# Output projection of a hybrid attention layer: four of eight pairs as two couples of seven block products

## The chip, the core and the metric

One core of a Trainium2 chip runs the kernel. The metric is the time of one execution on the device, in microseconds (us). The engines work in parallel, each through its own instructions in order: PE multiplies matrices (PEld loads its stationary operand), DVE and ACT do element work, POOL does too, SP issues most of the transfers (DMAs) between the chip's memory and the on-chip buffers. An instruction waits for semaphores that others raise; while it waits, everything behind it on its engine waits as well.

## The reference

A layer of 1024 rows (positions) and width 1024. The input is normalised and modulated, goes through one input projection, then through eight heads of forgetting attention and eight of stick-breaking attention; the gated head outputs `y` (1024 x 1024) go through the output projection, are multiplied by a gate per column, added to the scaled input and normalised. The part that the change touches:

```python
y = jnp.concatenate([y_fox, y_sb], axis=-1) @ w_out[layer]
resid = DEEPNORM_ALPHA * x + gate[:, None, :] * y
x = _layer_norm(resid, ln_g[layer], ln_b[layer])
```

## The kernel before

**Pairs and stages.** The sixteen heads are eight pairs; a pair is 128 of the 1024 inner columns of `y`. All large matmuls are done three times: each float operand is split into a rounded high part and the rest (`hi`, `lo`), and a product is yh by hi, yl by hi, yh by lo, summed in PSUM. A loop over 128 attention units (8 pairs, 2 heads, 8 blocks of 128 rows) writes the code; the matmuls of later projections are put between the units as fillers (`FILL` says how many steps for each pair), and in pair 7 the first output products are (`TAIL`). The order on each engine follows the order in which the code is written, with a few edges added (`after`).

**Weights.** `gen_split_out` runs beside the fillers from pair 4 on: for 16 pieces of `w_out` (128 x 512) it loads the piece, multiplies it by the gate on POOL, makes hi and lo on POOL (`fetch_w`, L125 and following) and stores both in `wo_dr`. `load_wo` loads them back when the last input projection lets go of the `u` and `v` buffers.

**The value buffers** (tag `v`, three of 8 KB per partition) hold the values of a pair's heads; at some times one of the three has no tenant.

**The tail.** Row tiles are taken in the order 6, 7, 4, 5, 2, 3, 0, 1, each in two halves of 512 columns (the last tile in 512, 256, 256). For one half, `o_step` (L937 to L939) adds the three products of all eight pairs in one PSUM accumulator (tag `acc`, two buffers). The y rows of pairs 0 to 6 were stored in `y_dr`; `load_y` reloads a row tile into `wraw` (two buffers, shared with weight pieces) and POOL makes hi (L917) and lo (L918) in the ring of five (`RING`). Pair 7 stays on chip (`y7h`, `y7l`). `o_half` then adds the scaled input on DVE (L956; `xr`, 512 KB, has four buffers of its own, tag `k`), takes the statistics (L957), and at the row's end `ln_finish` (L192 on DVE, L194 and L195 on POOL) and two DVE passes for each half (L964, L968) finish the row, which SP stores. The last tile shares the second pass with ACT and POOL (L971, L972).

Of the kernel before, what the change touches and what calls it, by code (L numbers as in the profile page):

```python
# [13 lines left out]
P = 128  # L14
# [13 lines left out]
def tile_hybrid_layer(  # L28
# [17 lines left out]
    nc = tc.nc  # L46

# [33 lines left out]
    SPACE = 10  # L81
    BEHIND = 1

# [26 lines left out]

    y_dr = dr.tile([NPAIR, P, SEQ], F32, tag="y_dr", name="y_dr")
    wo_dr = dr.tile([2, NPAIR, P, D], F32, tag="wo_dr", name="wo_dr")
# [4 lines left out]

    def ring_w(key):
        return [sb.tile([P, 528], F32R, tag=tag, bufs=RING, name=f"{tag}_{key}") for tag in ("whi", "wlo")]
# [26 lines left out]
    def load_x(t):  # L146
        if t == 6:
            late_x.append(pt_tile("x_67", F32))
        xi = att_tile(f"x_{t}") if t < 6 else late_x[0][:, t - 6, :]
        nc.sync.dma_start(xi, x[t * P:(t + 1) * P, :])  # L150
        xt.append(xi)
# [306 lines left out]
    masks, scaled, lows, gates = [], [], [], []  # L458
# [11 lines left out]
    def att_scores(u, following):  # L470
# [30 lines left out]
        else:  # L501
# [18 lines left out]
            nc.gpsimd.tensor_tensor(be[:, :ke - 1], be[:, :ke - 1], kp[:, 1:ke], op=ALU.mult)  # L520
# [24 lines left out]
    y_last, summed = [], []  # L545
# [15 lines left out]
    def att_sum(acc, p, h, j):  # L561
# [9 lines left out]
        if p == NPAIR - 1:  # L571
            if not y_last:
                y_last.extend([big("sg", 2, "y7h", F32R), big("kl", 2, "y7l", F32R)])
            yh, yl = y_last
            nc.scalar.copy(yh[r, qs], yt[r, :])
            nc.gpsimd.tensor_tensor(yl[r, qs], yt[r, :], yh.bitcast(F32)[r, qs], op=ALU.subtract)
        else:
            nc.sync.dma_start(y_dr[p, r, qs], yt[r, :])

# [303 lines left out]
    def load_wo(pr):  # L883
        hi = big(f"u{pr}", 1, f"woh_{pr}", F32R)
        lo = big(f"v{pr}", 1, f"wol_{pr}", F32R)
        nc.sync.dma_start(hi.bitcast(F32), wo_dr[0, pr])
        nc.sync.dma_start(lo.bitcast(F32), wo_dr[1, pr])
        wo[pr] = (hi, lo)

    def gen_split_out():  # L890
        for pr in range(NPAIR):
            for h in range(2):
                s = slice(h * 512, h * 512 + 512)
                with after(*scaled[BEHIND:BEHIND + 1]):
                    hi, lo = fetch_w(f"o{pr}_{h}", w_out[pr * P:(pr + 1) * P, s], 512, gate[:, s])
                nc.sync.dma_start(wo_dr[0, pr, :, s], hi.bitcast(F32)[:, :512])
                nc.sync.dma_start(wo_dr[1, pr, :, s], lo.bitcast(F32)[:, :512])
                for _ in range(SPACE):
                    yield
# [8 lines left out]
    y_t = {}  # L908

    def load_y(t):  # L910
        ts_ = slice(t * P, (t + 1) * P)
        for p0, n in ((0, 4), (4, 3)):
            raw = raw_tile(f"yr_{t}_{p0}")[:, :n * P]
            nc.sync.dma_start(raw.rearrange("p (a q) -> p a q", q=P),
                              y_dr[p0:p0 + n, :, ts_].rearrange("a p q -> p a q"))
            hi, lo = y_t[t, p0 // 4] = ring_w(f"y_{t}_{p0}")
            nc.gpsimd.tensor_scalar(hi[:, :n * P], raw, 1.0, 1.0, op0=ALU.mult, op1=ALU.mult)  # L917
            nc.gpsimd.tensor_tensor(lo[:, :n * P], raw, hi.bitcast(F32)[:, :n * P], op=ALU.subtract)  # L918

    o_acc = {}  # L920
    OUT_ORDER = (6, 7, 4, 5, 2, 3, 0, 1)

    def groups(t):
        return ((0, 512), (512, 768), (768, 1024)) if t == OUT_ORDER[-1] else ((0, 512), (512, 1024))

    def o_step(t, h, pr):
        if pr == 0:
            o_acc[t, h] = (t_tile if h == 2 else acc_tile)(f"o_{t}_{h}")
        acc = o_acc[t, h]
        if pr == NPAIR - 1:  # L930
            yh, yl = (v[:, t * P:(t + 1) * P] for v in y_last)
        else:
            yh, yl = (v[:, pr % 4 * P:][:, :P] for v in y_t[t, pr // 4])
        hi, lo = wo[pr]
        s = slice(*groups(t)[h])
        acc = acc[:, :s.stop - s.start]
        nc.tensor.matmul(acc, yh, hi[:, s], start=(pr == 0), stop=False)  # L937
        nc.tensor.matmul(acc, yl, hi[:, s], start=False, stop=False)  # L938
        nc.tensor.matmul(acc, yh, lo[:, s], start=False, stop=(pr == NPAIR - 1))  # L939

    res = {}

    def o_half(t, h):
        ts_ = slice(t * P, (t + 1) * P)
        s = slice(*groups(t)[h])
        ng = len(groups(t))
        if h == 0:
            xr = big("k", 4, f"xr_{t}")
            nc.sync.dma_start(xr, x[ts_, :])
            res[t] = (att_tile(f"r_{t}"), xr, sb.tile([P, 3, 6], F32, tag="st", bufs=3, name=f"st_b{t}")[:, :ng, :])  # L950
        r, xr, st = res[t]
        last = t == OUT_ORDER[-1]

        acc = o_acc[t, h][:, :s.stop - s.start]
        to = acc if last else r[:, s]
        nc.vector.scalar_tensor_tensor(to, xr[:, s], ALPHA, acc, op0=ALU.mult, op1=ALU.add)  # L956
        nc.vector.bn_stats(st[:, h, :], to)  # L957
        if h == ng - 1:
            mv, rs = ln_finish(st, f"b{t}")
            cuts = [slice(*g) for g in groups(t)]  # L960
            mid = [o_acc[t, j][:, :c.stop - c.start] if last else r[:, c] for j, c in enumerate(cuts)]

            def first(j):
                nc.vector.scalar_tensor_tensor(mid[j], mid[j], mv[:, 0:1], lgb[0][:, 0, cuts[j]],  # L964
                                               op0=ALU.subtract, op1=ALU.mult)

            def second(c, m):
                nc.vector.scalar_tensor_tensor(r[:, c], m, rs[:, 0:1], lgb[0][:, 1, c], op0=ALU.mult, op1=ALU.add)  # L968

            def shared(c, m):  # L970
                nc.scalar.activation(r[:, c], m, AF.Copy, scale=rs[:, 0:1])  # L971
                nc.gpsimd.tensor_tensor(r[:, c], r[:, c], lgb[0][:, 1, c], op=ALU.add)  # L972

            if not last:
                for j in range(2):
                    first(j)
                    second(cuts[j], mid[j])
                    if t not in OUT_ORDER[:2]:
                        nc.sync.dma_start(out[ts_, cuts[j]], r[:, cuts[j]])
                if t in OUT_ORDER[:2]:  # L980
                    nc.sync.dma_start(out[ts_, :], r)
                return
            for j in (1, 0, 2):
                first(j)
            shared(cuts[1], mid[1])
            c = cuts[2]
            cut = c.stop - 96
            shared(slice(cut, c.stop), mid[2][:, cut - c.start:])
            second(cuts[0], mid[0])
            second(slice(c.start, cut), mid[2][:, :cut - c.start])  # L990
# [4 lines left out]
    def gen_out_first(t):  # L995
        for h in range(2):
            for pr in range(NPAIR - 1):
                o_step(t, h, pr)
                yield
# [200 lines left out]
```

## Time and profile before

| what | value |
|---|---|
| median of 3 runs | 680.6 us (680.34 to 680.93) |
| span of the profiled execution | 678.6 us |
| median above that span | 2.0 us |
| POOL busy, 600 to 672 us | 29.48 us |
| DVE busy, 600 to 672 us | 41.30 us |

The span is the time from the first to the last event that the profiler recorded on the core; the device time adds a little around it. Busy times are in us; in a list of groups a row gives line, engine, operation, output and inputs, shape, count, then busy time, mean in ns, and idle time ahead with what ended it. A row of the timeline gives start, duration, engine, line and operation. In the list of transfers the last number is the median time from issue to landing.

### The profile page before, as it was taken

To read this page: it belongs to the slowest core of one execution; us is meant where nothing else is said; L and a number is where in the kernel's file an instruction comes from. 1 tells how busy PE (TensorE), PEld (TensorE's weight loads), DVE (VectorE), ACT (ScalarE), POOL (GpSimd) and SP (SyncE) were. 2 spreads that over 40 slices of the span, in tenths; PEclk is the share of its full clock that TensorE was granted. 3 is DMA by queue.
4 is the path that set the end of the run, shared out by engine and by line. 5 is a ranking of instruction groups with operands and counts; after the bars stand their busy time and mean duration, and the time that the engine had idled before them with its cause. 6 is when DMAs were issued, how large, how long until landed. Compare 5 with 4: busy or idle time off the path is not lost.

```text
span 678.6 us, 11231 instructions
## 1 busy us (share of the span) xinstructions
PE 668.3 (98%) x3713; PEld 571.2 (84%) x3713; DVE 485.9 (72%) x1001; ACT 382.6 (56%) x889; POOL 405.2 (60%) x530
## 2 busy tenths in 40 slices
PE   8999999999999999999999999999999999999995
PEld 4888898888998888889988888889988888888885
DVE  6787779868677777686776675766676777775645
ACT  5576468757567667576675564655565766521000
POOL 5560279755357556556378878785785365655412
PEclk9999999999999999999999999999999999999998
DMA  9983432112101112122124555263452297153301
GB/s 326 401 312 126 139 79 75 41 28 67 29 20 56 54 42 57 40 54 56 49 93 144 151 164 174 87 201 112 127 169 59 70 350 302 59 177 107 120 32 63
DMA packets 46474, 81.55 MB, mean 120 GB/s; under 512 B 5264, under 2 KB 20176, under 8 KB 46416
## 3 DMA queue, kind: packets, MB, share of 16 engines
q1 hardware_dynamic: 44832, 76.37, 35.1%
q10 hardware_dynamic: 1584, 4.47, 2.1%
q8 instruction: 29, 0.48, 0.3%
q14 instruction: 29, 0.24, 0.1%
HBM read 60.34 MB, written 16.29 MB: 113 GB/s over the span
## 4 chain that ended last, share of the span: by engine, by line
PE 97%; DMA 1%; DVE 0%; POOL 0%; ACT 0%; issue 0%; SPq 0%; POOLq 0%
PE m L312 11%; PE m L314 10%; PE m L313 10%; PE pv L554 10%; PE T L537 9%; PE S L484 5%; PE S L483 5%; PE o L939 4%; PE o L937 4%; PE o L938 4%; PE v L370 4%; PE v L372 4%; PE v L371 4%; PE st_q L647 1%; PE st_k L647 1%; PE st_late L647 1%
## 5 line engine op out<-in xcount | busy, mean ns | idle before, releaser
L540 DVE TENSOR_TENSOR pt<-T,pt 128x512 fp32r<-128x512 f32 (+2 forms) x192 | 102.7, 553 | 43.8 <-ACT pt L539 42.2
L539 ACT CAST pt<-T 128x512 fp32r<-128x512 f32 (+2 forms) x192 | 88.9, 479 | 64.5 <-PE T L537 62.5
L312 PE MATMUL m<-uh,whi 128*128 128x512 f32 x304 | 123.3, 405 | 0.1
L314 PE MATMUL m<-uh,wlo 128*128 128x512 f32 x304 | 119.8, 394 | 0.0
L313 PE MATMUL m<-ul,whi 128*128 128x512 f32 x304 | 119.7, 394 | 0.0
L520 POOL TENSOR_TENSOR be<-be,kp 128x127 f32<-128x127 f32 (+3 forms) x64 | 78.9, 1234 | 36.2 <-DVE kp L518 24.4
L554 PE MATMUL pv<-pt,v 128*128 128x512 f32 x320 | 82.8, 388 | 0.0
L514 DVE TENSOR_TENSOR_SCAN kp<-kp,floor 128x128 f32<-128x128 f32 (+3 forms) x64 | 58.6, 915 | 17.6 <-ACT kp L506 17.4
L499 POOL TENSOR_SCALAR a<-a,l 128x1024 f32<-128x1024 f32 (+3 forms) x64 | 48.4, 756 | 34.3 <-DVE l L497 26.0
L483 PE MATMUL S<-k,q 128*128 128x512 f32 (+5 forms) x192 | 68.8, 360 | 0.0
L314 PEld LDWEIGHTS m<-uh,wlo 128*128 128x128 f32 x304 | 57.1, 188 | 13.7
L496 ACT ACTIVATE a<-a,nm 128x1024 f32<-128x1024 f32 (+3 forms) x64 | 49.8, 779 | 28.6 <-DVE nm L491 28.1
L312 PEld LDWEIGHTS m<-uh,whi 128*128 128x128 f32 x304 | 57.2, 188 | 10.2 <-PE T L537 0.3
L484 PE MATMUL S<-kl,qz 128*128 128x512 f32 (+5 forms) x192 | 65.2, 341 | 0.0
L313 PEld LDWEIGHTS m<-ul,whi 128*128 128x128 f32 x304 | 57.3, 188 | 9.0
L554 PEld LDWEIGHTS pv<-pt,v 128*128 128x128 f32 x320 | 55.5, 189 | 8.9
L570 POOL TENSOR_TENSOR ty<-ty,sg 64x256 f32<-64x256 f32 x64 | 46.9, 733 | 23.4 <-issue 12.2
L491 DVE CUSTOM_DVE_ANT_0 a<-S,fb 128x1024 f32<-128x1024 f32 (+3 forms) x64 | 48.2, 753 | 16.9 <-PE S L484 12.0
L456 ACT CAST qz<-q 64x128 fp32r<-64x128 f32 x128 | 37.3, 296 | 34.2 <-PE S L484 33.0
L506 ACT ACTIVATE kp<-S 128x384 f32<-128x384 f32 (+4 forms) x96 | 44.0, 494 | 21.5 <-PE S L484 20.2
L370 PE MATMUL v<-whi_v,uh 128*128 128x256 f32 (+1 forms) x192 | 54.7, 285 | 0.0
L372 PE MATMUL v<-wlo_v,uh 128*128 128x256 f32 (+1 forms) x192 | 54.2, 282 | 0.0
(296 smaller groups left out, 1628.3 us busy)
## 6 DMA issues: line engine op xcount, KB each, us to landing
raw<-in_w_qkg_dram SPq DMA_DIRECT2D x38, 256.0 KB, 2.7
wss<-in_w_ss_dram SPq DMA_DIRECT2D x14, 512.0 KB, 8.1
x<-in_x_dram SPq DMA_DIRECT2D x8, 512.0 KB, 7.1
k<-k SPq DMA_DIRECT2D x32, 128.0 KB, 2.3
wg<-in_w_gate_dram SPq DMA_DIRECT2D x8, 512.0 KB, 4.9
raw_o<-in_w_out_dram SPq DMA_DIRECT2D x16, 256.0 KB, 3.0
fb<-f_dr ACTq DMA_DIRECT2D x8, 512.0 KB, 4.5
wo_dr<-whi_o SPq DMA_DIRECT2D x16, 256.0 KB, 2.1
```

The source lines that it names most:

```text
L312: nc.tensor.matmul(acc, hi[:, c], u_hi[kt][:, s], start=(kt == 0), stop=False)
L313: nc.tensor.matmul(acc, hi[:, c], u_lo[kt][:, s], start=False, stop=False)
L314: nc.tensor.matmul(acc, lo[:, c], u_hi[kt][:, s], start=False, stop=(kt == NB - 1))
L370: nc.tensor.matmul(acc[:, :n], u_hi[kt][:, ts_], hi[:, s], start=(kt == 0), stop=False)
L372: nc.tensor.matmul(acc[:, :n], u_hi[kt][:, ts_], lo[:, s], start=False, stop=(kt == NB - 1))
L483: nc.tensor.matmul(S[:, s, :w], qst[p][h][:, qs], kst[p][h][:, ks], start=True, stop=False)
L484: nc.tensor.matmul(S[:, s, :w], z, klo[p][:, ks], start=False, stop=True)
L520: nc.gpsimd.tensor_tensor(be[:, :ke - 1], be[:, :ke - 1], kp[:, 1:ke], op=ALU.mult)
L537: nc.tensor.transpose(tp[:, b * P:(b + 1) * P], a[:, kb * P:(kb + 1) * P], ident)
L539: nc.scalar.copy(hi[:, :n, qo:qo + P], t3)
L540: lows[:] = [nc.vector.tensor_tensor(lo[:, :n, qo:qo + P], t3, hi.bitcast(F32)[:, :n, qo:qo + P], op=ALU.subtract)]
L554: nc.tensor.matmul(acc2[:, :, q0:], vt[p][:, kb, h * P:(h + 1) * P], pt[:, :, q0:], start=(kb == 0), stop=(kb == last))
```

## The change

Pairs 0 to 3 become two couples. Within a couple, y of a pair of row tiles is a 2 x 2 block matrix A (row tile by pair), the gated weights a 2 x 2 block matrix B (pair by column half), and the 2 x 2 result is had by seven block products instead of eight, from sums and differences of blocks:

- the early products A11 B11, S2 T2, S3 T3, S1 T1, each into an accumulator of its own over both couples; ACT and DVE add them up in an SBUF tile `e_t` of each row;
- the late products P4 = A22 T4, P2 = A12 B21, P3 = S4 B22, each in one accumulator with the plain products of pairs 4 to 7 for that half (12 matmuls); the half that gets no late product is `gen_22`.

The row pairs are (6,7), (4,5), (2,3), (0,1), numbered 0 to 3. The operands (S and T blocks, hi and lo) are made by `gen_operands` in the value buffer without tenant, in the fill steps that `ROOMS` names, which are steps of pairs 2 and 3 for couple 0 and of pairs 4 and 5 for couple 1, and are stored in `wo_dr`, `ye_dr`, `yl_dr`. `gen_plain` splits the weights of pairs 4 to 7 as before (eight pieces). Each half's residual is now a load of 256 KB into `wraw`, a scaling on ACT and an add on POOL into `e_t`; the accumulator is added on DVE (`half_add`). A finished row is stored as one piece of 512 KB, and for its first half ACT and POOL make the second pass (`shared`). The y rows of pairs 4 to 6 are loaded as before, three blocks of 128 for a row tile instead of seven; rows 7, 5 and 3 at set steps, rows 6, 4, 2, 1, 0 behind all late loads.

```diff
-    SPACE = 10
+    STAY = 14
+    SPACE = 12
+    ROOMS = ((126, 226), (264, 366))
+    NC = 2
+    ROWS = ((6, 7), (4, 5), (2, 3), (0, 1))
+    EARLY = (("A11", "B11"), ("S2", "T2"), ("S3", "T3"), ("S1", "T1"))
+    LATE = {"P4": ("A22", "T4"), "P2": ("A12", "B21"), "P3": ("S4", "B22")}
...
+    def ring_set(key):
+        return sb.tile([P, 2, 528], F32R, tag="w", bufs=RING, name=f"w_{key}")
...
+    def halves(raw, n, key):
+        both = rooms[now()][:, 2:]
+        nc.scalar.copy(both[:, 0, :n], raw[:, :n])
+        with tied():
+            nc.gpsimd.tensor_tensor(both[:, 1, :n], raw[:, :n], both.bitcast(F32)[:, 0, :n], op=ALU.subtract)
+        return both.bitcast(F32)
...
+    def weight_piece(c, q):
...
+            nc.gpsimd.tensor_tensor(r4, r4, both, op=ALU.mult)
...
+        both = halves(raw, 3 * P, f"ob_{c}_{q}")
...
+        less(b11, b12, b11)
+        less(b12, b22, b12)
+        less(b22, b22, b11)
+        less(b21, b21, b22)
+        yield
+        both = halves(raw, 4 * P, f"ot_{c}_{q}")
...
+    def load_y(row):
+        n = NPAIR - 1 - 2 * NC
+        raw = raw_tile(f"yr_{row}")[:, :n * P]
...
+        hi, lo = y_row[row] = ring_w(f"y_{row}")
+        nc.gpsimd.tensor_scalar(hi[:, :n * P], raw, 1.0, 1.0, op0=ALU.mult, op1=ALU.mult)
+        nc.gpsimd.tensor_tensor(lo[:, :n * P], raw, hi.bitcast(F32)[:, :n * P], op=ALU.subtract)
...
+    def residual(t, x, h):
+        r = ROWS[t][x]
+        xr = raw_tile(f"xr_{t}_{x}_{h}")[:, :512]
+        nc.sync.dma_start(xr, x_in[r * P:(r + 1) * P, h * 512:h * 512 + 512])
+        nc.scalar.activation(xr, xr, AF.Copy, scale=ALPHA)
+        nc.gpsimd.tensor_tensor(half_of(t, x, h), half_of(t, x, h), xr, op=ALU.add)
...
+    def half_add(t, x, h, acc):
+        e = half_of(t, x, h)
+        nc.vector.tensor_tensor(e, e, acc, op=ALU.add)
+        stats(t, x, h, e)
...
+    def row_end(t, x):
+        r, row = e_t[t][x], ROWS[t][x]
+        mv, rs = ln_finish(o_st[t, x][:, :2, :], f"b{t}{x}")
+        for h in range(2):
+            c = slice(h * 512, h * 512 + 512)
+            first(r[:, c], c, mv)
+            (shared if h == 0 else second)(r, c, r[:, c], rs)
+        nc.sync.dma_start(out[row * P:(row + 1) * P, :], r)
...
+    def gen_late(t, which, x, h):
+        residual(t, x, h)
+        acc = (t_tile if which == "P2" else acc_tile)(f"o_{t}_{which}")
+        yield from block(t, 1, LATE[which], acc, ends=(True, False))
+        yield from plain(t, x, slice(h * 512, h * 512 + 512), acc, ends=(False, True))
+        half_add(t, x, h, acc)
+        if which != "P2":
+            row_end(t, x)
...
-    tail = chain([gen_out_first(6), gen_out_last(6)] + [gen_out(t) for t in OUT_ORDER[1:]])
+    tail = chain([gen_early(0), gen_early(1), gen_22(0), gen_22(1), gen_early(2), gen_early(3), gen_22(2),
+                  *(gen_late(t, "P4", 1, 0) for t in range(3)),
+                  gen_late(0, "P2", 0, 0), gen_late(1, "P2", 0, 0),
+                  gen_late(0, "P3", 0, 1), gen_late(1, "P3", 0, 1),
+                  gen_late(2, "P2", 0, 0), gen_late(2, "P3", 0, 1),
+                  gen_22(3), gen_late(3, "P4", 1, 0), gen_late(3, "P2", 0, 0), gen_end(3)])
...
+        if k == LAST + 15:
...
+            for row in (6, 4, 2, 1, 0):
+                load_y(row)
```

**What the order of the instructions says.** POOL in the middle of the tail, before (`whi_y` and `wlo_y` are the split y rows, `rs_b5` the reciprocal root of row tile 5):

```order
L570 TENSOR_TENSOR ty_7_1_0_7446<-ty_7_1_0_7446,sg_7_6538 64x256
L917 TENSOR_SCALAR whi_y_0_0_7493<-yr_0_0_7491 128x512
L576 TENSOR_TENSOR y7l_6798<-ty_7_1_0_7446,y7h_6797 64x256
L918 TENSOR_TENSOR wlo_y_0_0_7494<-yr_0_0_7491,whi_y_0_0_7493 128x512
L194 TENSOR_SCALAR rs_b5_7469<-mv_b5_7467 128x1
L195 TENSOR_TENSOR rs_b5_7469<-rs_b5_7469,mhalf_89 128x1
```

The same place after (`w_y_1` is the split y row tile 1, `xr_0_1_0` the residual of row pair 0, second row, first half; `e0_1` the sum tile of that row, `rs_b01` its reciprocal root):

```order
L1058 TENSOR_SCALAR w_y_2_7456<-yr_2_7454 128x384
L1059 TENSOR_TENSOR w_y_2_7456<-yr_2_7454,w_y_2_7456 128x384
L1058 TENSOR_SCALAR w_y_1_7461<-yr_1_7459 128x384
L1059 TENSOR_TENSOR w_y_1_7461<-yr_1_7459,w_y_1_7461 128x384
L1100 TENSOR_TENSOR e0_1_6897<-e0_1_6897,xr_0_1_0_7488 128x512
L215 TENSOR_SCALAR rs_b01_7515<-mv_b01_7513 128x1
L216 TENSOR_TENSOR rs_b01_7515<-rs_b01_7515,mhalf_89 128x1
L1100 TENSOR_TENSOR e1_1_7071<-e1_1_7071,xr_1_1_0_7524 128x512
L1120 TENSOR_TENSOR e0_1_6897<-e0_1_6897,lngb_6698 128x512
```

The adds of residuals (L1100) and the shared second pass (L1120) are new on POOL, and the first residual of the late group stands behind the split of row 1.

SP, the transfers at that place, after (`yr_` are y rows, `xr_` residuals, both in `wraw`):

```order
L1055 DMA yr_2_7454<-y_dr_91 128x3x128
L1055 DMA yr_1_7459<-y_dr_91 128x3x128
L1055 DMA yr_0_7464<-y_dr_91 128x3x128
L1098 DMA xr_0_1_0_7488<-in_x_dram 128x512
L1098 DMA xr_1_1_0_7524<-in_x_dram 128x512
L1098 DMA xr_2_1_0_7564<-in_x_dram 128x512
L1129 DMA out_0_dram<-e0_1_6897 128x1024
```

The residuals of the late group are issued behind all five y rows, in the same two buffers: xr_0_1_0 in that of yr_1, xr_1_1_0 and the next two in that of xr_0_1_0, until yr_0 is split.

DVE, after, at the end of the first late products (`o_0_P4` is an accumulator):

```order
L1109 TENSOR_TENSOR e0_1_6897<-e0_1_6897,o_0_P4_7492 128x512
L1105 BN_STATS st_b01_7238<-e0_1_6897 128x6
L213 BN_AGGR mv_b01_7513<-st_b01_7238 128x2
L1113 SCALAR_TENSOR_TENSOR e0_1_6897<-e0_1_6897,mv_b01_7513,lngb_6698 128x512 x2
L1116 SCALAR_TENSOR_TENSOR e0_1_6897<-e0_1_6897,rs_b01_7515,lngb_6698 128x512
L1109 TENSOR_TENSOR e1_1_7071<-e1_1_7071,o_1_P4_7528 128x512
```

Before, the first of these six was L956, which took the residual straight from its own buffer. Now the add that frees an accumulator stands behind the second pass of the row ahead, and it reads an `e` tile to which POOL has added the residual.

Late in the tail on POOL, after (`rs_b10` belongs to row pair 1, first row, whose sum tile is `gate`):

```order
L215 TENSOR_SCALAR rs_b10_7725<-mv_b10_7723 128x1
L1100 TENSOR_TENSOR e3_0_7346<-e3_0_7346,xr_3_0_0_7852 128x512
L216 TENSOR_TENSOR rs_b10_7725<-rs_b10_7725,mhalf_89 128x1
L1120 TENSOR_TENSOR gate_88<-gate_88,lngb_6698 128x512
```

A residual of the last row pair stands between the two operations of a root that an earlier row waits for.

More of the change, by code (lines that the diff above doesn't have):

```diff
@@ L578, in att_sum @@
             nc.sync.dma_start(y_dr[p, r, qs], yt[r, :])
+            stored.add((p, h, j))
     def chain(gens):
@@ new lines, in tied, with less, now @@
+    def tied():
+        return after(*(scaled[BEHIND:BEHIND + 1] or prods))
+    def halves(raw, n, key):
[4 more added lines that the diff above has]
+        return both.bitcast(F32)
+    def less(to, a, b, op=ALU.subtract):
+        nc.vector.tensor_tensor(to, a, b, op=op)
+    rooms, handed = {}, [0]
+    def now():
+        return [i for i, (a, b) in enumerate(ROOMS) if a <= done[0] < b][0]
@@ L941, in tile_hybrid_layer @@
[L941 to L990, printed above, removed]
-            nc.scalar.dma_start(out[ts_, cuts[0]], r[:, cuts[0]])
-            rest = slice(cuts[1].start, c.stop)
-            nc.sync.dma_start(out[ts_, rest], r[:, rest])
```

318 lines of the change are left out of this document (242 added, 76 removed).

## Prediction

> **What bounds the kernel now.** The page comes first, for the busy shares and the chain; then the busy time by stage, to see whether the chain's answer holds in each stage; then the waits of PE.
>
> ```profile
> span 678.6 us, 11231 instructions
> PE 668.3 (98%) x3713; PEld 571.2 (84%) x3713; DVE 485.9 (72%) x1001; ACT 382.6 (56%) x889; POOL 405.2 (60%) x530
> PE 97%; DMA 1%; DVE 0%; POOL 0%; ACT 0%; issue 0%; SPq 0%; POOLq 0%
> ...
> 219.00:311.00 92.00, 92.00 (x478) 77.40 (x477) 70.97 (x109) 62.57 (x144) 56.92 (x80) 1.00 0.20 50
> 349.00:440.00 91.00, 91.00 (x466) 76.40 (x465) 61.49 (x154) 52.02 (x121) 73.32 (x82) 1.00 0.44 134
> 600.00:672.00 72.00, 71.46 (x336) 58.72 (x334) 41.30 (x73) 4.13 (x13) 29.48 (x37) 1.00 0.27 95
> ...
> PE sc_all L179 <- POOL ident masks.py:199: 1.5, 1, 1.5
> PE xT_early L256 <- ACT x L222: 0.9, 1, 0.9
> PE st_q L647 <- ACT uh L270: 0.4, 1, 0.4
> ```
>
> PE makes 97% of the chain. In the stage rows (window, length, then busy us of PE, PEld, DVE, ACT, POOL, then clock) it is busy all the time, in the attention stages as in the output projection; in the last window the missing half microsecond is only the time after the last matmul. Its list of waits is three entries long, all in the start. So a matmul that goes is worth its whole time, and any new wait of PE costs its whole length: nothing is slack.
>
> **What the products save.** Before, the projection has 360 matmuls of 512 columns and 48 of 256; after, 342 and 36 (a couple takes 7 block products of 3 matmuls for a pair of row tiles where two pairs took 8). So 18 of 512 and 12 of 256 go.
>
> ```profile
> 619.25 0.39 PE L937 MATMUL o<-woh,whi_y 128*128 128x512 f32 x1
> 619.48 0.40 PE L938 MATMUL o<-woh,wlo_y 128*128 128x512 f32 x1
> 619.72 0.40 PE L939 MATMUL o<-wol,whi_y 128*128 128x512 f32 x1
> ...
> 620.65 0.39 PE L937 MATMUL o<-woh,whi_y 128*128 128x512 f32 x1
> ...
> 670.35 0.28 PE L938 MATMUL o<-woh,wlo_y 128*128 128x256 f32 x1
> ...
> 671.18 0.28 PE L939 MATMUL o<-wol,y7h 128*128 128x256 f32 x1
> ```
>
> A matmul's duration (0.39) overlaps the next one; the price is from start to start: 1.40 over the six steps from 619.25 to 620.65, 0.233 each, and 0.83 over the seven from 670.35 to 671.18, 0.1186 each for 256 columns. 18 x 0.233 + 12 x 0.1186 = 4.19 + 1.42 = **5.6 us saved**. The last matmul starts at 671.18 and the span ends at 678.6; that ending of 7.4 us has the same operations in both kernels, so it is carried over.
>
> **First stall: the residual halves share a two-buffer pool with the y rows.** The tail's n-th matmul stands after the change where the n-th stood before, so the times above are also those that the new one would have if it waited for nothing. The third product of the late group (o_2_P4) would start at 620.65. It needs the accumulator of o_0_P4, which DVE frees with the add into e0_1; that add follows POOL's add of the residual xr_0_1_0; its transfer follows, in its buffer, yr_1, which POOL frees with its two operations on w_y_1; and these write the ring set that held row 5, last read by the ninth plain matmul of o_1_P4. That one stands at 619.72 and ends at 620.11. So the chain starts half a microsecond before PE needs its end.
>
> ```profile
> 611.36 0.39 PE L939 MATMUL o<-wol,whi_y 128*128 128x512 f32 x1
> ...
> 611.84 0.51 POOL L917 TENSOR_SCALAR whi_y<-yr 128x384 fp32r<-128x384 f32 x1 [2.49 <-PE o L939]
> 612.44 1.01 POOL L918 TENSOR_TENSOR wlo_y<-yr,whi_y 128x384 fp32r<-128x384 f32 x1
> ...
> raw<-in_w_qkg_dram SPq DMA_DIRECT2D x38, 256.0 KB, 2.7
> xr<-in_x_dram SPq DMA_DIRECT2D x8, 512.0 KB, 3.5
> out_dram<-r SPq DMA_DIRECT2D x11, 256.0 KB, 2.0
> ...
> L633 ACT CAST hw<-raws 128x512 fp32r<-128x512 f32 x5 | 3.1, 623 | 3.3 <-DMA raws<-in_w_qkg_dram 3.3
> L125 POOL TENSOR_TENSOR raw_o<-raw_o,gate 128x512 f32<-128x512 f32 x16 | 20.7, 1294 | 6.6 <-DMA raw_o<-in_w_out_dram 6.6
> L956 DVE SCALAR_TENSOR_TENSOR r<-xr,o 128x512 f32<-128x512 f32 x14 | 9.5, 686 | 19.2 <-PE o L939 18.6 <-POOL whi_y L917 0.5
> ```
>
> The same release exists before: matmul at 611.36, end 611.75, POOL's copy at 611.84, so 0.09 us for the hop, 0.51 and 1.01 for the two operations with 0.09 between. Then the transfer, 256 KB: 2.7 us to landing for the like load of weights (between 2.0, that of an output store, and 3.5, the 512 KB load); ACT's scaling 0.62; POOL's add 1.29; DVE's add 0.69; three hops of 0.09. Sum: 0.09 + 0.51 + 0.09 + 1.01 + 2.7 + 0.62 + 1.29 + 0.69 + 0.27 = 7.3, from 620.11 to 627.4, and the signal to PE makes it 627.5. Against 620.65 that is **6.9 us of idle PE** (6.2 to 7.7 with the two other transfers). Behind POOL's wait for w_y_1 stand all later POOL operations of the tail, so nothing of this can be overtaken.
>
> The Trainium skill, "DMA: Bandwidth & Descriptors" (Anatomy of one DMA), says that a transfer has about 2 us of fixed cost, mostly the receipt of its last byte. The rows agree, with 2.0 us for 256 KB as the shortest; by 2 us alone the stall would be 6.2.
>
> **Second stall: one turn of a buffer is longer than a product.** A product of 18 matmuls takes 18 x 0.233 = 4.2 us. Thirteen halves still need their residual then, one for each product of the late group; a turn of its buffer is 2.7 + 0.62 + 1.29 and hops, 4.8 us. Until POOL has split w_y_0, the other buffer is taken by yr_0, so four residuals go through a single buffer, one every 4.8 us. POOL also carries, per row, two operations on the reciprocal root and one shared add, and runs them in order.
>
> ```profile
> L964 DVE SCALAR_TENSOR_TENSOR r<-r,mv_b,lngb 128x512 f32<-128x512 f32 x14 | 10.9, 818 | 0.2
> L968 DVE SCALAR_TENSOR_TENSOR r<-r,rs_b,lngb 128x512 f32<-128x512 f32 x14 | 10.1, 748 | 3.2 <-POOL rs_b L195 3.2
> L194 POOL TENSOR_SCALAR rs_b<-mv_b 128x1 f32<-128x1 f32 x8 | 4.9, 607 | 22.7 <-DVE mv_b L192 21.6 <-DVE l L497 0.8
> L195 POOL TENSOR_TENSOR rs_b<-rs_b,mhalf 128x1 f32<-128x1 f32 x8 | 6.7, 831 | 0.6
> ```
>
> I followed the engines' orders by these durations from POOL's first residual add, done at 626.7: the adds for rows' halves end at 631.5, 636.2, 641.7, 644.6, 647.2, 649.4, 652.0, 654.2, 656.7, 659.3, 661.4. The last of these (e3_0) stands ahead of the power operation for row 10's root; DVE's second pass over `gate` waits for that (662.2 to 662.95), and the add that frees o_2_P3's accumulator stands behind it on DVE: done 663.7. o_3_P4 takes that accumulator. After the first stall PE would reach it 140 instructions after 627.5, at 660.1. The working gives 3.6 us; with 0.1 us for each of the some eight hops that I left out, 4.5. I take **4.4 us**. The bounds are 2 (transfers of 2.2 us) and 6 (of 3.0): some eight transfers follow one another, and each adds its difference.
>
> **Smaller terms.** All have a gain excluded, since PE has no idle time that they could take away, so they start at nothing. (a) o22_3 waits for the add of o_1_P3: 0.25. (b) The last early product of each row pair is read by two DVE adds of 0.69, the next but one product may start only behind them, and one product of 6 matmuls is 1.4 long: 0 to 0.5, taken 0.3. (c) T4's second weight block is loaded where the last score product's k buffer was (its matmuls end at 606.0) and is read at 612.86.
>
> ```profile
> 605.76 0.27 PE L484 MATMUL S<-kl,qz 128*128 128x128 f32 x1
> woh<-wo_dr SPq DMA_DIRECT2D x8, 512.0 KB, 8.1
> ```
>
> Alone such a 512 KB load takes 3.5 us, in a queue of them 8.1, so 0 to 1.3; taken 0.3. (d) The operand pieces in pairs 2 and 3 add to POOL, for the eight pieces of a couple, 4 x 1.29 + 8 x 1.02 + 8 x 1.30 = 23.7 us, to DVE 32 operations, to ACT 16 casts.
>
> ```profile
> L918 POOL TENSOR_TENSOR wlo_y<-yr,whi_y 128x384 fp32r<-128x384 f32 x6 | 6.1, 1020 | 0.4
> L379 DVE TENSOR_TENSOR v<-v,v 128x128 fp32r<-128x128 f32 x60 | 17.0, 285 | 8.8 <-ACT v L378 8.0
> ```
>
> By the window 219 to 311, POOL goes from 56.9 to 80.6 of 92 us and DVE (32 x 0.285 = 9.1) from 71.0 to 80.1: it fits, but a unit whose weights pass through POOL's in-order queue may come up to 1.3 us late. 0 to 3, taken 0.45, as most pieces are tied behind the unit's own operation. In pairs 4 and 5, POOL loses eight of the sixteen split pieces and gains the same 23.7: nothing. Together (a) to (d): **1.3 us**.
>
> **The clock.** An idle PE has a price of its own. In the tail the granted clock falls soon after the last matmul, and the first matmuls of the program, of one form, are slower than the later ones:
>
> ```profile
> 670.00:675.00 5.00, 1.46 (x13) 1.25 (x11) 3.40 (x8) 0.82 (x2) 1.58 (x4) 0.85 0.00 0
> 675.00:679.00 4.00, 0.00 (x0) 0.00 (x0) 0.18 (x1) 0.00 (x0) 0.26 (x1) 0.50 0.35 133
> L179 PE MATMUL sc_all<-ident 128*128 128x512 f32 x8 | 5.1, 802 | 1.5 <-POOL ident masks.py:199 1.5
> L179 PE MATMUL sc_all<-ident x8: 592/648/1222, 1.5 to 6.1; 128*128 128x512 f32 x8
> ```
>
> 0.85 over five microseconds is 1.5 us at half clock, so it fell about 2 us after PE stopped. The eight first matmuls are busy for 5.1 us, against 8 x 0.592 = 4.7 if all were as fast as the fastest (0.4 more), and by their mean they are 8 x (0.802 - 0.592) = 1.7 longer; so a restart costs 0.4 to 1.7 us. After the first stall that loss is made up, because the residual chain runs on and PE waits for it at o_3_P4 anyway; after the second it is not: 0 to 1.7, **0.8 taken**.
>
> The Trainium skill, "TensorE: Matmul & The Clock Gate" (The HAM clock gate), speaks against every gap: PE falls to half clock after an idle window of about 3.4 us and needs about 3.4 us of work to come back. The rows of the end agree on the fall, to 0.50. By that rule both stalls would be followed by half speed, the sum that the third rival below takes.
>
> **Sum.** 678.6 - 5.6 + 6.9 + 4.4 + 1.3 + 0.8 = 686.4 us of span; the median of the runs shown, 680.6, lies 2.0 above the profiled span, so **688.4 us**, slower by 1.1%.
>
> **Rivals.**
> - *Only the first stall is seen.* If transfers land in 2.2 us and the hops are short, the residuals catch up with PE: 680.6 - 5.6 + 6.4 + 1.1 = 682.5. For it: out stores of the same size land in 2.0. Against: every load row is at 2.7 or more, and POOL's own sequence is nearly as long as PE's.
> - *The block products come through.* One mechanism: the ring set of row 5 is free before o_1_P4 reads it, so w_y_1 is split some 7 us earlier. Then stall one is gone and the residual chain is 7 us ahead, which covers stall two: 680.6 - 5.6 + 1.3 = 676.3. It decides whether POOL's copy into w_y_1 starts before or after 620. Against: row 5's set has its second reader in that product, and the order has nothing between.
> - *The clock halves after both stalls*, and the second restart follows a longer gap: 1.7 for each in place of 0.8 gives 688.4 + 2.6 = 691.0. For it the fall at the end; against it, that the first loss hides in the second wait.
> - *The attention stage becomes bound by POOL* in pairs 2 and 3 (88% busy): term (d) at 3 in place of 0.45: 691.0. Against: 11 us are left.
>
> **How the numbers follow.** Forecast 0.55 (685 to 690.5 by its bounds), first rival 0.2, second 0.06, third 0.12, fourth 0.07. The range leaves out the second rival, the low part of the first and the high part of the last two: 682.0 to 692.0. A measurement of this kernel can tell about 0.2% (1.4 us) from no change. Faster by more: 0.06. Within: 0.05, the low end of the first rival, where saving and stall cancel. Slower: 0.89.
>
> **What would show it.** Right: the list of PE's waits gets an entry of 6 to 7 us on the first matmul of o_2_P4, released by DVE's add into e0_1, and one of 2 to 6 us on o_3_P4; POOL's copy for w_y_1 starts just after the ninth plain matmul of o_1_P4; the granted clock dips near 625. Wrong: those matmuls start without a wait; the residual transfers land in far less than 2.7 us; or PE waits between 219 and 440 for transposes of weights that POOL was late with.

## The result and the profile after

| | before | after |
|---|---|---|
| median | 680.47 us | 724.61 us (722.17 to 725.97, 4 runs) |
| ratio | | 1.0645, 95% interval 1.0623 to 1.0668 |
| span of the profiled execution | 678.6 us | 720.2 us |

The change makes the kernel 6.5% slower; forecast were 1.1%. First the page of the changed kernel (span, busy shares, engines on the chain that ended last), then its list of what PE waited for (total, times, longest):

```profile
span 720.2 us, 11511 instructions
PE 677.8 (94%) x3683; PEld 573.1 (80%) x3683; DVE 529.1 (73%) x1074; ACT 414.2 (58%) x948; POOL 442.2 (61%) x553
PE 61%; POOL 12%; DMA 9%; DVE 7%; issue 6%; ACT 4%; SPq 1%; POOLq 0%; ACTq 0%; DVEq 0%
...
PE T L558 <- DVE pt L561: 12.0, 8, 3.5
PE o_P L1073 <- DVE e L1109: 11.4, 2, 7.2
PE pv L575 <- DVE pt L561: 5.2, 2, 4.1
```

Before, PE had three waits, all in the start. Now it makes 61% of the chain, and two kinds of wait stand out: 11.4 us in two waits of the tail, the two that were forecast, and 17.2 us for DVE's copies of transposed weights (L561), in the attention stages, where next to nothing was forecast. Where the time goes is seen by comparing the start of the same instruction in both traces. The last score product of all starts here at 635.73, before at 605.76, so 30.0 us are lost by then; the last matmul starts at 712.56 against 671.18, so 41.4 are lost by then and the tail alone costs 11.4:

```profile
635.73 0.28 PE L505 MATMUL S<-kl,qz 128*128 128x128 f32 x1
...
712.56 0.28 PE L1089 MATMUL o_end<-wo_v,y7h 128*128 128x256 f32 x1
```

**The tail** went nearly as worked out. The timeline of the changed kernel around the first wait (start, duration, engine, line, operation; in brackets the idle time ahead and what ended it):

```profile
651.15 0.40 PE L1089 MATMUL o_P<-wo_v,y7h 128*128 128x512 f32 x1
...
651.20 0.51 POOL L1058 TENSOR_SCALAR w_y<-yr 128x384 fp32r<-128x384 f32 x1
651.80 0.99 POOL L1059 TENSOR_TENSOR w_y<-yr,w_y 128x384 fp32r<-128x384 f32 x1
...
652.82 5.51 SPq L1098 DMA_DIRECT2D xr<-in_x_dram  x2
...
655.98 0.63 ACT L1099 ACTIVATE xr<-xr 128x512 f32<-128x512 f32 x1 [6.92 <-DMA xr<-in_x_dram]
656.69 1.26 POOL L1100 TENSOR_TENSOR e<-e,xr 128x512 f32<-128x512 f32 x1 [3.90 <-ACT xr L1099]
...
657.98 0.69 DVE L1109 TENSOR_TENSOR e<-e,o_P 128x512 f32<-128x512 f32 x1 [8.59 <-POOL e L1100]
658.73 0.79 PE L1073 MATMUL o_P<-wt,late_u 128*128 128x512 f32 x1 [7.18 <-DVE e L1109]
...
697.17 0.80 PE L1073 MATMUL o_P<-wt,late_u 128*128 128x512 f32 x1 [4.18 <-DVE e L1109]
```

From the split of row 1 on, the transfer, ACT, POOL, DVE, PE are link for link the chain of the forecast, 7.18 us where 6.9 were worked out, then 4.18 where 4.4 were. Only the head is another: the split of row 1 began when POOL was through with row 2 (651.20), whose load had landed late, and not when PE let go of the ring set. The ninth plain matmul of o_1_P4 starts at 650.46 and is over at 650.85, so this makes 0.3 us.

**The attention stages.** By the same comparison, 0.3 us are lost at what was 224 us, 12.8 at 325 (in pairs 2 and 3 the operands of couple 0 are made), still 12.8 at 343, 24.1 at 455 (pairs 4 and 5, couple 1), still 24.1 at 558, then 30.0 at the last score product of pair 7. One stretch at the end of the first 12.8, the sums and differences of operands (L936) on DVE, what POOL does then, ACT's next rounding (L930) and PE:

```profile
316.33 4.64 DVE L936 TENSOR_TENSOR room<-room 128x128 f32<-128x128 f32 x4
...
317.55 2.00 POOL L541 TENSOR_TENSOR be<-be,kp 128x1023 f32<-128x1023 f32 x1
...
321.05 0.62 ACT L930 CAST room<-room 128x512 fp32r<-128x512 f32 x1 [5.00 <-DVE room L936]
...
322.31 0.63 PE L558 MATMUL T<-ident,be 128*128 128x128 f32 x4 [2.94 <-DVE pt L561]
```

ACT stands 5.0 us at a rounding, DVE's four short operations take 4.64 us, and the copies of transposed weights stand behind both. Which of the engines sets this was not to be read off; the experiments were made for it.

### The profile page after: what moved, and what is told of

It is laid out like the page before. It is cut to its first block, busy times and chain, and to the rows that moved or that the text cites. A ratio compares the mean times of both kernels' runs of the same rounds, so it can differ in the third digit from the quotient of the medians.

```text
span 720.2 us, 11511 instructions
## 1 busy us (share of the span) xinstructions
PE 677.8 (94%) x3683; PEld 573.1 (80%) x3683; DVE 529.1 (73%) x1074; ACT 414.2 (58%) x948; POOL 442.2 (61%) x553
## 4 chain that ended last, share of the span: by engine, by line
PE 61%; POOL 12%; DMA 9%; DVE 7%; issue 6%; ACT 4%; SPq 1%; POOLq 0%; ACTq 0%; DVEq 0%
PE pv L575 7%; PE T L558 6%; PE m L333 5%; PE m L335 4%; PE m L334 4%; PE v L391 4%; PE v L393 4%; PE v L392 4%; PE S L505 3%; PE S L504 3%; DVE room L936 3%; POOL room L932 2%; POOL e L1100 2%; DMA xr<-in_x_dram 2%; POOL be L541 2%
## 5 line engine op out<-in xcount | busy, mean ns | idle before, releaser
L561 DVE TENSOR_TENSOR pt<-T,pt 128x512 fp32r<-128x512 f32 (+2 forms) x192 | 102.9, 552 | 45.7 <-ACT pt L560 44.0
L333 PE MATMUL m<-uh,w 128*128 128x512 f32 x304 | 123.8, 407 | 0.0
L335 PE MATMUL m<-uh,w 128*128 128x512 f32 x304 | 120.2, 395 | 0.0
L334 PE MATMUL m<-ul,w 128*128 128x512 f32 x304 | 120.1, 395 | 0.0
L335 PEld LDWEIGHTS m<-uh,w 128*128 128x128 f32 x304 | 57.4, 189 | 13.8
L575 PEld LDWEIGHTS pv<-pt,v 128*128 128x128 f32 x320 | 55.7, 190 | 14.7 <-DVE pt L561 5.7
L517 ACT ACTIVATE a<-a,nm 128x1024 f32<-128x1024 f32 (+3 forms) x64 | 49.8, 778 | 28.7 <-DVE nm L512 28.2
L333 PEld LDWEIGHTS m<-uh,w 128*128 128x128 f32 x304 | 57.4, 189 | 10.2 <-PE T L558 0.3
L334 PEld LDWEIGHTS m<-ul,w 128*128 128x128 f32 x304 | 57.6, 189 | 9.0
L591 POOL TENSOR_TENSOR ty<-ty,sg 64x256 f32<-64x256 f32 x64 | 47.2, 738 | 23.3 <-DVE ty L590 12.5
L391 PE MATMUL v<-w_v,uh 128*128 128x256 f32 (+1 forms) x192 | 56.0, 292 | 0.0
L392 PE MATMUL v<-w_v,ul 128*128 128x256 f32 (+1 forms) x192 | 55.4, 288 | 0.0
L393 PE MATMUL v<-w_v,uh 128*128 128x256 f32 (+1 forms) x192 | 55.2, 288 | 0.0
```

What stands on the lines that cost most here:

```text
L333: nc.tensor.matmul(acc, hi[:, c], u_hi[kt][:, s], start=(kt == 0), stop=False)
L334: nc.tensor.matmul(acc, hi[:, c], u_lo[kt][:, s], start=False, stop=False)
L335: nc.tensor.matmul(acc, lo[:, c], u_hi[kt][:, s], start=False, stop=(kt == NB - 1))
L391: nc.tensor.matmul(acc[:, :n], u_hi[kt][:, ts_], hi[:, s], start=(kt == 0), stop=False)
L392: nc.tensor.matmul(acc[:, :n], u_lo[kt][:, ts_], hi[:, s], start=False, stop=False)
L393: nc.tensor.matmul(acc[:, :n], u_hi[kt][:, ts_], lo[:, s], start=False, stop=(kt == NB - 1))
```

## The experiments

Each ran once, beside a run of the kernel before on the same chip (680.1 to 680.5 us). The middle columns give how late score products start against the trace of before, at what were 325, 455 and 606 us there; for the change they are of its profiled execution, which took 722.2 us. The kernels e3, e4 and e5 have the attention code of the change, so their rows show the scatter of single executions: 11.9 to 13.4 at 325, 24.1 to 27.6 at 455. Differences of 2 to 3 us between two rows mean nothing.

| kernel | 325 | 455 | 606 | time, us |
|---|---|---|---|---|
| the change | 12.8 | 24.1 | 30.0 | 724.6 |
| e1 no operand arithmetic | 0.1 | 3.3 | 8.4 | 700.4 |
| e2 roundings on POOL | 24.0 | 40.0 | 51.5 | 742.4 |
| e3 rows 1 and 0 late | 11.9 | 25.4 | 31.2 | 713.8 |
| e4 residual on DVE | 13.1 | 26.8 | 27.2 | 707.0 |
| e5 rows late, residual mixed | 13.4 | 27.6 | 27.9 | 710.6 |
| e6 interleaved | 8.9 | 22.1 | 27.1 | 719.2 |
| e7 first parts in the ring | 21.8 | 35.6 | 41.3 | 733.1 |
| e8 both | 18.1 | 34.0 | 39.1 | 730.1 |
| e9 without ACT's part | 10.6 | 23.7 | 31.4 | 724.5 |
| e10 without DVE's part | 1.1 | 11.8 | 17.9 | 709.8 |
| e11 without POOL's part | 8.5 | 21.0 | 23.3 | 716.7 |
| e12 roundings on DVE | 18.2 | 33.9 | 39.6 | 729.5 |
| e13 DVE's load alone (it ran before 100 us) | 3.1 | 12.0 | 18.4 | 710.0 |
| e14 DVE's waits alone | 10.8 | 20.3 | 25.2 | 717.0 |
| e15 POOL's part alone | 0.3 | 12.3 | 18.0 | 710.1 |
| e16 e1 and e5's tail | 0.0 | 4.7 | 5.0 | 688.5 |
| e17 stores from elsewhere | 14.7 | 22.1 | 28.7 | 719.0 |
| e18 e15 and e17's stores | 6.7 | 7.3 | 13.0 | 700.4 |

**Is it the operand work at all?** e1 keeps the transfers and drops `less`, the gate product and `halves`.

```diff
-        nc.scalar.copy(both[:, 0, :n], raw[:, :n])
...
-            nc.gpsimd.tensor_tensor(both[:, 1, :n], raw[:, :n], both.bitcast(F32)[:, 0, :n], op=ALU.subtract)
...
-        nc.vector.tensor_tensor(to, a, b, op=op)
```

> Left out: the arithmetic on the operands (gate product, rounding, rest, sums and differences); all their transfers stay, so the output is not the reference's. In the changed kernel the last score product stands 30 us later than before: 24 us are lost by the end of pair 5 and 5.5 more in pair 7. Theory 'operand work' (the new operations hold up the attention's, by their queues or by their load): the 24 us go, 724.6 - 24 = 700.6 us (698 to 703), with the wait of 3.5 us in pair 7 and the two in the tail as they are. Rival 'transfers' (the 20 MB more of traffic slow down others' transfers or the engines' memory): hardly a change, over 718 us.

700.4 us: the arithmetic makes 20.8 of the 24.1 us, the traffic by itself at most 3.3.

**First idea: the roundings stand in ACT's queue.** e2 moves them to POOL (`nc.gpsimd.tensor_scalar` in place of `nc.scalar.copy`), e12 to DVE (`nc.vector.tensor_copy`), e9 leaves them out.

> The 32 roundings of operands go from ACT to POOL, ahead of the subtraction there. Theory 'ACT's queue' (a rounding waits on ACT for DVE or for a transfer, and the copies of transposed weights stand behind it): at least half of the 24 us go, 712 us or less, though POOL has 16 us more to do over pairs 2 to 5. Rival 'load' (POOL's and DVE's busy time is too much): POOL, already 24 us fuller in pairs 2 and 3, is fuller still, and the time rises above 728 us. Between these, both have a part.

> Nothing left out: the 32 roundings on DVE instead of ACT, each in DVE's order behind the differences that it needs. Theory 'ACT's queue': ACT has no operand work and DVE waits less than ACT did: 712 us or less. Rival 'load of DVE' (80 of 92 us in pairs 2 and 3, with some 8 more 88): 726 us or more, as when the roundings went to POOL.

> Left out: ACT's 32 roundings of operands alone (the high parts stay zero); the rest as in the changed kernel, with one clearing of the room by DVE. Without any operand arithmetic (e1_no_operand_math) 3.3 us were lost by the end of pair 5 instead of 24.1, so 20.8 us are to be divided. Theory 'ACT's queue' (attention's copies stand behind roundings that are not ready): nearly all of it goes, 708 us or less. Rival 'POOL's and DVE's load': 718 us or more.

742.4, 729.5 and 724.5 us. The idea falls: without any rounding the time is the same. (e2 lost 15.5 us at one place, where the matmuls of the next values waited for the buffer in which POOL was still making operands.)

**More distance between the steps.** e6 advances a weight and a y piece in turns; the pieces then overwrite each other's parts before they are stored, so the operands are not the reference's. e7 takes `ring_set(key)` for the first parts, e8 does both.

> The same operand work, but a weight piece and a y piece advance in turns, so that four fill steps instead of two lie between an operation and the one that needs it. Busy times do not change. Theory 'queues' (ACT and DVE stand at operand operations that are not ready, attention's copies behind them): the 24 us of the changed kernel fall to 12 or less, 712 us or less. Rival 'load': 722 us or more. Against the first speaks that the two pieces share one pair of buffers for high part and rest, so a rounding may wait for the other piece's transfer.

> The first rounding and rest of each piece go to a set of the weight ring, so that the second rounding need not wait for the first one's transfer. Theory 'queues, by transfers': the waits of ACT for operand transfers go, 716 us or so. Rival 'queues, by DVE' (ACT stands at the second rounding because DVE's differences are not there, 21 of its 31 us of waits at operand roundings): 722 us or more. If the weights' prefetch suffers from the ring's lost set, above 726 us with PE waiting for weights.

> Both: turns of a weight and a y piece, and first parts in the ring. Theory 'queues': now neither DVE's differences nor transfers are late when ACT reaches a rounding; the 24 us fall to 6 or less, 706 us or less. Rival 'load': 722 us or more.

719.2, 733.1, 730.1 us. In e6 ACT's roundings wait no longer for DVE's sums, and 22.1 us are still lost at 455. Why e7 and e8 are slower than the change is not shown; in e7 the first roundings of y pieces stand 16.7 us for loads of y.

**One engine's part at a time.**

> Left out: DVE's 64 sums and differences of operand blocks alone. Theory 'ACT's queue': ACT no longer waits for DVE at the second roundings (21 us of its waits, not all of them worth PE time), only for transfers and POOL: 708 to 714 us. If DVE's own stand behind POOL's subtractions counts, it is in this too. Rival 'POOL's load': 720 us or more.

> Left out: POOL's operand work alone (16 gate products, 32 subtractions; 47 us of busy time). DVE and ACT then wait for nothing but each other and the transfers. Theory 'ACT's queue': about half of the 20.8 us stays, 712 us, since roundings still stand behind DVE and transfers. Rival 'POOL's load': all goes, 704 us or less.

In pairs 2 and 3 DVE's 32 operations carry all but 1.1 of the 12.8 us, though ACT waited for them and POOL did most of the work. In pairs 4 and 5 neither part is enough.

**DVE: its time or its waits?** e13 does a statistics operation of the same length on a constant in place of each sum; e14 keeps the operation and its dependences, for one column (`to[:, :1]`).

> Left out: the 64 sums and differences, as in e10_no_dve; in the place of each DVE does an operation of the same length (statistics of a 128x128 constant) that waits for nobody and for which nobody waits. Without the sums 1.1 us were lost by the end of pair 3, with them 12.8. Theory 'DVE's queue' (DVE stands at a difference until POOL has subtracted, ACT stands at the second rounding until DVE has come to it, attention's work behind both): as e10_no_dve, 709 to 712 us, at most 3 us lost by the end of pair 3. Rival 'DVE's load' (9.1 us more in 92): 718 us or more, 8 us or more lost by the end of pair 3.

> Left out: all but one column of each sum and difference, so DVE has 64 short operations with all their waits and those who wait for them. Theory 'DVE's queue': most stays, 718 us or more, 8 us or more lost by the end of pair 3. Rival 'DVE's load': 712 us or less.

e13 does not answer the question. Its statistics wait for nobody, so they ran far ahead of the operand stages. The list of one line's instructions gives count, durations (min/median/max in ns), first and last start:

```profile
L937 DVE BATCH_NORM_STATS2 st_free<-ident x64: 236/277/296, 49.8 to 87.9; 128x6 f32<-128x128 f32 x64
```

They cost some 2 us there, and from 224 to 325 e13 loses 0.9 us, like e10 (0.7), which has no sums at all. e14 does answer: its operations are little more than half as long when nothing holds them, and 10.8 of the 12.8 us stay. So most of the loss is not their own length. The same list for DVE's operand operations, first in the changed kernel, then in e14:

```profile
L936 DVE TENSOR_TENSOR room<-room x64: 257/293/3374, 227.2 to 466.2; 128x128 f32<-128x128 f32 x64
```

```profile
L936 DVE TENSOR_TENSOR room<-room x64: 127/161/3239, 227.2 to 459.7; 128x1 f32<-128x1 f32 x64
```

An operation on one column took up to 3.2 us while it ran. And most of it is not a wait for a semaphore: in pairs 2 and 3 (219 to 345 us) the 32 operations of the change took 23.7 us of DVE, where 285 ns each would be 9.1, and DVE sat idle ahead of them for 1.7:

```profile
L936 DVE TENSOR_TENSOR room<-room 128x128 f32<-128x128 f32 x32 | 23.7, 739 | 1.7 <-POOL room L932 1.2
```

Where a long one ends is seen in the changed kernel's timeline, in two places, DVE's row and then POOL's:

```profile
236.25 1.37 DVE L936 TENSOR_TENSOR room<-room 128x128 f32<-128x128 f32 x1
...
236.18 1.29 POOL L149 TENSOR_TENSOR w<-raw,w 128x512 fp32r<-128x512 f32 x1
...
304.31 2.67 DVE L936 TENSOR_TENSOR room<-room 128x128 f32<-128x128 f32 x2 [0.21 <-POOL room L932]
...
304.20 0.76 POOL L591 TENSOR_TENSOR ty<-ty,sg 64x256 f32<-64x256 f32 x1
...
304.93 1.57 POOL L541 TENSOR_TENSOR be<-be,kp 128x767 f32<-128x767 f32 x1
```

POOL's operation ends at 237.47, DVE's at 237.62. Of the two from 304.31 (together 2.67, the second some 0.3) the first stands behind two of POOL's: the one that ran when it began, over at 304.96, and the multiplication behind that, over at 306.50. So a DVE operation whose two inputs are both in SBUF stands until POOL's running operation is over, and at times for POOL's next one too. In the whole trace 26 of the 64 took over 0.4 us; each of these ended 0.13 to 0.16 us after an operation of POOL, and three of them stood behind two. The Trainium skill, "SBUF — State Buffer" (Who interferes with whom), says that a DVE instruction with two SBUF inputs contends with a GpSimd instruction that reads SBUF, the loser blocked for the whole instruction, and that DVE with at most one SBUF input, outside its two-port modes, does not. The rows agree: L400, an addition of the same shape with one input in PSUM, keeps its 286 ns beside the same POOL work, and L936 takes 616 in the mean:

```profile
L400 DVE TENSOR_TENSOR v<-v,v 128x128 fp32r<-128x128 f32 x17 | 4.8, 286 | 2.6 <-ACT v L399 2.3
L936 DVE TENSOR_TENSOR room<-room 128x128 f32<-128x128 f32 x64 | 39.4, 616 | 7.4 <-POOL room L932 6.7
```

It also explains why e11 gained little in pairs 2 and 3. Attention's own POOL operations, the longest of all, were still there to stand behind, and the sums (L934 in e11, 219 to 345 us) still took 610 ns in the mean:

```profile
L934 DVE TENSOR_TENSOR room<-room 128x128 f32<-128x128 f32 x32 | 19.5, 610 | 1.0 <-DMA room<-in_w_out_dram 0.2
```

No run keeps the sums and takes this conflict away (by an input in PSUM, say), so how many of the 12.8 us are its own was not measured: that the sums bring nearly all of them is shown by e10, that most is not their length by e14, and that they stand behind POOL by the trace.

**Pairs 4 and 5.** e15 leaves POOL's part alone; e17 and e18 store from `gate` (`kept` for `both` in the stores), so that nobody waits until a store has read the one shared pair of buffers.

> Left out: DVE's and ACT's operand work; POOL's stays with its transfers. In pairs 4 and 5 no single engine's part, left out alone, helped (11.3 us lost as it is; 10.7 without DVE's, 13.1 without ACT's, 12.5 without POOL's; 3.2 without all). If POOL's queue by itself holds up attention there (the split of value weights came late without DVE's part): 708 us or more, 7 us or more lost between the ends of pairs 3 and 5. If it takes two engines that wait for each other: 703 us or less.

> POOL's operand work alone (as in e15_pool_alone) and the stores from the gate tile. There 0.2 us were lost in pairs 2 and 3 and 12.0 in pairs 4 and 5. Theory 'stores': at most 4 stay in pairs 4 and 5, 703 us or less. Rival 'POOL's load': 9 or more stay, 708 us or more.

> All operand arithmetic and all transfers stay, but the operand stores take their data from the gate tile (so the operands in memory are wrong): no rounding or subtraction has to wait until a store has read the shared pair of buffers. Theory 'stores' for pairs 4 and 5 (whichever engine writes the shared buffers first stands until their store is out, with the attention's work behind it): of the 11.3 us lost between the ends of pairs 3 and 5, 5 or less stay; the 12.8 up to the end of pair 3, which came from DVE's waits, stay above 8: 715 to 719 us. Rival 'POOL's load' for pairs 4 and 5: 9 us or more stay there, 722 us or more.

POOL's part alone loses 12.0 us here, and 0.6 when the stores read elsewhere (from 6.7 at 325 to 7.3 at 455), at the same POOL work. What POOL waited for at its operand subtractions in e15:

```profile
POOL room L931 <- DMA wo_dr<-room: 13.5, 7, 3.0
POOL room L931 <- DMA ye_dr<-room: 6.2, 3, 3.2
```

So there POOL stood at the stores, and attention's scaling and the split of value weights behind it. In the whole kernel ACT stands at one as well, and PE's longest wait of the attention stages is behind it:

```profile
472.62 0.62 ACT L930 CAST room<-room 128x512 fp32r<-128x512 f32 x1 [5.77 <-DMA ye_dr<-room]
...
474.39 1.01 PE L575 MATMUL pv<-pt,v 128*128 128x512 f32 x2 [4.13 <-DVE pt L561]
```

With the stores elsewhere the whole kernel (e17) loses 7.4 us here, against 11.3 in the change and 13.5 to 14.2 in e3 to e5, so this is worth 4 to 7 us. One reservation: in e17 and e18 the stores, freed of what they waited for, ran between 102 and 156 us, which cost 4.7 and 3.5 us by 224 (e18 lost another 3 in pair 2) and took their traffic out of these stages. That traffic alone is not the cause is shown by e1, which has it (for couple 1 between 358 and 405 us) and loses 3.2.

**The tail.** e3 puts `load_y(1)` and `load_y(0)` behind the third P4 product. e4 replaces ACT's scaling and POOL's add by one DVE operation in `half_add`; e5 does that for second rows of row pairs 0 to 2, with e3's rows.

```diff
-            for row in (6, 4, 2, 1, 0):
+            for row in (6, 4, 2):
...
+        nc.vector.scalar_tensor_tensor(e, x_half[t, x, h], ALPHA, e, op0=ALU.mult, op1=ALU.add)
```

> Rows 1 and 0 of y are loaded and split after the third P4 product instead of ahead of the late group, so that the residuals of P4 need not wait for ring set and buffer. Theory 'chain through the shared buffers': the wait of 7.2 us on the third P4 product goes, and with it half-clock time worth 1.7; if the later wait of 4.2 us (and 3.0 of half clock) came only from the late start of the same chain, that goes too: 724.6 - 16.1 = 708.5 us; if a buffer's turn is too long by itself, 715.7 us. Rival (the transfers of the residuals are slow wherever they start): over 722 us.

> The residual is no longer scaled on ACT and added on POOL, but scaled and added in one DVE operation behind the add of the accumulator. Theory 'chain': a turn of a buffer loses ACT's 0.62 and POOL's 1.29 and gains DVE's 0.69; the wait on the third P4 product goes from 7.2 to about 6, the later one (4.2, with 3.0 of half clock) to nothing, and the wait of 3.5 us in pair 7 (ACT stood at a residual's transfer; 1.7 of half clock behind it) goes: 724.6 - 1.2 - 7.2 - 5.2 = 711 us. Rival (DVE, with 0.7 us more per product, becomes the bound of the tail): 720 us or more.

> Rows 1 and 0 late (as in e3_rows_late), and the residuals of the second rows of the first three row pairs, which are the earliest seven but one, scaled and added on DVE; all later ones on ACT and POOL. Theory (the tail's waits are the shared buffers' chain, and the wait in pair 7 is ACT standing at a residual's transfer): the last score product is 24 to 27 us late, as the operand work alone makes it, and the tail then runs at PE's pace, 5.6 us shorter than before but 0.7 for a late weight block: 680.1 + 25.5 - 4.9 = 701 us (699 to 704). Rival (DVE is the tail's bound, as in e4_residual_on_dve, where it was busy without a gap from 660 to 698): 707 us.

> Left out: the operand arithmetic, as in e1_no_operand_math; and the tail as in e5_tail_mixed. If the two losses are independent, the times add: 700.4 - (724.6 - 710.6) = 686.4 us (684 to 688), with the last score product 3 to 5 us late and the tail itself 2 us longer than before. If the tail's waits depend on the attention's state: away from that by 3 us or more.

713.8: the first wait went from 7.2 us to 1.8, the second from 4.2 to 3.0, so the first was the chain, and a second chain stays. 707.0, where 711 were expected: all waits of the tail but 1.4 and 0.7 are gone. The first was to stay at about 6 us; it went because DVE there adds the accumulator ahead of the residual, so that the accumulator comes free without waiting for it. The 5.9 us of pair 7 are gone as well. Now DVE is the bound, busy 29.93 of 30 us, and the span ends 10.0 us behind the last matmul instead of 7.6:

```profile
660.00:690.00 30.00, 28.64 (x124) 22.88 (x123) 29.93 (x46) 3.62 (x5) 14.43 (x16) 1.00 0.47 167
```

710.6 is 9.6 us off the 701 expected: o_3_P4 waits 4.9 us, behind the ends of five rows that DVE and POOL finish between 660 and 690. 688.5 is 2 us above the 686.4 of independent losses. No version tried is faster than the kernel before.

## Why the prediction was wrong, step by step

- *5.6 us saved*: borne out by the tail's sum. 11.4 = -5.6 + 7.2 + 4.2 + 0.6 + half-clock time of 4.7 comes to 11.1.
- *First and second stall, 6.9 and 4.4*: 7.2 and 4.2, by the links named but for the head of the first (0.3 us). e3 and e4 show the cause by taking it away.
- *Smaller terms (a) to (c)*: (c) was 0.58 for 0.3; (a) and (b) are not in PE's list.
- *The clock, 0.8*: mis-sized. Five times the clock fell to half, by the record for 3.4 us each time in the attention stages and for 6.8 us from the first stall on and again from the second, of which 3.7 and 6.2 us lie behind the restart. Rows of the stretches (the last but two number is the mean clock):

```profile
324.00:328.00 4.00, 4.00 (x23) 4.00 (x22) 2.90 (x7) 2.33 (x7) 3.03 (x5) 0.57 0.64 205
655.00:663.00 8.00, 4.27 (x11) 3.41 (x12) 3.76 (x6) 1.87 (x3) 4.19 (x4) 0.57 0.12 39
696.00:704.00 8.00, 6.83 (x17) 5.38 (x18) 6.05 (x9) 1.73 (x3) 5.34 (x5) 0.57 0.20 81
```

Against 0.233 us from start to start, the matmuls behind the two restarts lost 1.8 and 2.9 us, 4.7 in the tail. By half of 3.4 us each, the three dips before it cost 5.1. The third rival was right that the clock halves behind both stalls, at 1.7 us each.
- *Term (d), the operand pieces, 0.45 us (bounds 0 to 3)*: **this step failed**: 24.1 us. It added up busy times, which fit, and allowed for POOL alone being late. It priced DVE's operations, 64 over both couples, by L379 (285 ns), whose one input is in PSUM; with both inputs in SBUF they stand behind POOL's operations, and 18 us of work became 39.4 us of DVE. It also asked only of POOL what stands behind an operation that comes late, not of DVE and ACT. "In pairs 4 and 5 ... nothing" failed by the stores: the shared pair of buffers has each rounding and subtraction wait for a transfer. The fourth rival had the place right, but the cause (POOL's load) wrong, and a price of 3 us.
- *Nothing in pair 7*: 5.9 us, a step left out. A residual's scaling stood on ACT until its transfer was there, with the attention's exponentials behind it:

```profile
582.82 0.63 ACT L1099 ACTIVATE xr<-xr 128x512 f32<-128x512 f32 x1 [4.80 <-DMA xr<-in_x_dram]
...
585.92 0.63 PE L558 MATMUL T<-ident,a 128*128 128x128 f32 x4 [3.46 <-DVE pt L561]
```

e4 and e5, where this residual is not ACT's, lose 0.4 and 0.3 us from 455 to 606. This queue was named for POOL in the prediction, never for ACT.
- What stays open: how much of the 12.8 us in pairs 2 and 3 a kernel without the conflict of DVE and POOL would keep; how the 7.4 us of e17 in pairs 4 and 5 divide between DVE and ACT; and the 3.3 us of e1, which follow a wait for POOL's scaling.

## What to carry to other kernels

Side work in a stage that has no slack is not priced by adding busy times: for each added instruction ask what it waits for, which of the stage's own instructions stand behind it in that engine's order, and whether its operands put it in conflict with another engine. A price row must have the same kinds of operands, not only the same shape. Here a saving of 0.8% of PE's work did not pay for new work on three engines that were 56 to 72% busy beside a PE that never waited.

## What the runs showed of the hardware

- Of the 64 DVE operations of the change with two SBUF inputs (L936), 26 took over 0.4 us, up to 3.4, and each of these ended 0.13 to 0.16 us after an operation of POOL did. Their own length mattered little: 3.2 us for one column (e14).
- The clock fell to half behind single idle times of PE from 1.88 us (e6) and 1.93 us (e7) up, behind all of 3.3 us and more, and not behind others of 2.40, 2.65, 3.00 and 3.27 us (e9, e14, e18, e12); it came back after 3.4 us or a multiple.
- Two operand stores of 256 and 128 KB, issued at 465.56 and 466.17 us, landed 6.6 and 6.3 us later, beside other traffic; the medians of their like in the same execution are 2.7 and 2.4.
